# Hymba decoder step: the verdict among the last multiplications, the general pass on SyncE's queue, the first norm's squares behind the first four products

## The chip, the cores and the metric

One core of a Trainium2 chip runs the whole program in one launch. The metric is the device time of a run in microseconds (us). The engines are TensorE (PE; its weight loads are listed as PEld), VectorE (DVE), ScalarE (ACT), GpSimd (POOL) and SyncE (SP, which here only issues transfers). An engine's name with a q (POOLq, SPq) stands for its sequencer: branches, semaphores, register loads, DMA issues.

## The reference

A decoder layer for 264 token columns (a prompt of 256 and 8 single new tokens), model width 2048, all in float32:

```python
h = h + 0.5 * swiglu(rmsnorm(h, norm_ffn1), ffn1_gate, ffn1_up, ffn1_down)
mix, C_f, n_f, m_f, buf = mixing_block(rmsnorm(h, norm_mix), w_in, b_gates, ...)
h = h + mix
h = h + 0.5 * swiglu(rmsnorm(h, norm_ffn2), ffn2_gate, ffn2_up, ffn2_down)
y = rmsnorm(h, norm_final)
```

with `swiglu(x, wg, wu, wd) = (silu(x @ wg) * (x @ wu)) @ wd` (inner width 5504) and `rmsnorm(x, g) = x * rsqrt(mean(x*x) + 1e-6) * g`. The mixing block is a chunkwise mLSTM with four heads beside a gated short convolution. Outputs are y and the new states.

## The kernel before, in words

**Layout.** Activations lie transposed: the 2048 features are 16 blocks of 128 partitions, `h[0]` to `h[15]`, each 128 x 264 float32; two neighbours share one tile, `hpair[i]`, 128 x 528. Every large product goes through the weights in pieces of up to 8 blocks of 128 x 128 (512 KB of float32).

**Two passes.** `hymba_step` records the program twice. The first pass splits each float32 operand into two float16 parts and takes three products per block (`three`, L224 to L226: high·high, high·low, low·high). It also keeps sums that tell whether the numbers stayed in float16's range: `watch` reduces 16 columns of each product into a column of `stat`, `watch_norm` reduces each norm's sums into `squares`, and `judge` compares them with bounds. The single number `bad` is loaded by all five engines (L109); if it is not 0, the second, general pass is run (L110). With these inputs it is skipped: each engine takes the branch over the general pass's instructions.

**A weight piece's way.** `fetch` issues the load on SP's queue (`wraw`), ACT rounds it to float16 (`whi`, L178), DVE makes the rest (`wlo = wraw - whi`, L186), and PE takes both. Six buffers each stand between them; `product` keeps five pieces ahead. Nothing is reordered by a scheduler: instructions stand on each engine in the order in which the code is written (`manual_schedule`), except that `at(n, f)` puts `f` off by n steps of `tick`, of which each product makes two (its start and its half).

**The start.** The first four products (gate and up of blocks 0 and 1) are taken together by `products4` while x arrives: nine groups, two with one feature block and seven with two; a group of two holds 2 x 4 x 3 = 24 matmuls. `ahead` loads a group's h, cuts x = h·gain into two float16 parts (ACT then DVE, 264 columns each), and squares h for the first norm: even blocks on ACT (L376), odd ones on POOL (L378), summed on POOL into `acc` (L382). After the four products `norm.finish` sums `acc` over the partitions with a matmul against ones (L353), `rsqrt` makes the norm's factor, and DVE scales the finished products by it. Here F0 to F8 name the nine groups, and W9, W10, ... the 512 KB pieces behind them, two to a product.

**The end.** `ffn("2")` closes with 16 down products. After each, `done(kb)` adds to the final norm's squares; the last calls `nf.finish`. Then DVE multiplies the 16 blocks of h by the factor (L480), SP stores them (L482, L484), and behind that come `watch_norm`, two `judge`s, the matmul of the verdicts (L492) and the cast to `bad` (L497). A program ends with a barrier of all engines (L1066): SP waits there for all transfers, POOL gathers the others and clears the semaphores.

**Queues.** Weights, h and y go by SP's queue, `h[0]` and `vecs` by ACT's. The small transfers of the mixing block and `bg` are issued by POOL (software-driven queue), in both passes.

Of the kernel before, what the change touches and what calls it, by code (L numbers as in the profile page):

```python
# [8 lines left out]
F32 = mybir.dt.float32  # L9
F32R = mybir.dt.float32r  # L10
F16 = mybir.dt.float16
AF = mybir.ActivationFunctionType
# [3 lines left out]
KB = D // 128  # L16
# [98 lines left out]
def step(ctx: ExitStack, tc: tile.TileContext, a: dict, bad=None):  # L115
# [6 lines left out]
    AHEAD = 5 if half_size else 2  # L122

# [16 lines left out]
    nc.gpsimd.dma_start(bg, a["bg"])  # L140
# [142 lines left out]
    if half_size:  # L283
        stat = const.tile([128, NSTAT], F32, name="stat")
        nc.gpsimd.memset(stat, 2.0 * SUMS[0])
        squares = const.tile([128, 8], F32, name="squares")
# [69 lines left out]
    class Norm:  # L356
# [5 lines left out]
        def block(self, kb, by_act=False):  # L362
            self.cut(kb)
            self.square(kb, by_act)
# [7 lines left out]
        def square(self, kb, by_act=False):  # L372
            new = self.acc is None
            sq = t264("acc", 1) if new else t264("sq")
            if by_act:
                nc.scalar.activation(sq, h[kb], AF.Square)  # L376
            else:
                nc.gpsimd.tensor_tensor(sq, h[kb], h[kb], op=ALU.mult)  # L378
# [14 lines left out]
    def ffn(layer, norm, done, start=None):  # L393
        with tc.tile_pool(name=f"act_{norm.tag}", bufs=1) as apool:
            first = True
            for half, blocks in enumerate(HALVES):
                act = {}
                for i, j in enumerate(blocks):
                    if start is not None and j < 2:
                        if j == 0:  # L400
                            ps4 = start()
                        pg, pu = ps4[2 * j : 2 * j + 2]
                    else:
                        pg = product((layer, "g", j), norm.x, range(KB))
                        pu = None
# [8 lines left out]
                    if pu is None:  # L414
                        pu = product((layer, "u", j), norm.x, range(KB))
# [19 lines left out]
    def ahead(part):  # L435
# [5 lines left out]
        for kb in range(k0, k0 + n):  # L441
            n1.block(kb, kb % 2 == 0)
# [9 lines left out]
        bank=bank, at=at, tick=tick, watch=watch, high=high, low=low, PART=PART, s3=s3,  # L452
# [6 lines left out]
    def done(kb):  # L459
# [12 lines left out]
    def judge_early():  # L472
        early.append(len(stats))
        judge(stat[:, : early[0]], SUMS)

# [9 lines left out]

    if half_size:
        watch_norm(nf.ssum)
        judge(stat[:, early[0] : len(stats)], SUMS)
        judge(squares, SQUARES)
        ps = bank()[:1, :1]  # L490
        for i, v in enumerate(verdicts):
            nc.tensor.matmul(  # L492
                ps, v, ones[:, :1], start=(i == 0), stop=(i == len(verdicts) - 1)
            )
        some = const.tile([1, 1], F32, name="some")
        nc.vector.tensor_scalar(some, ps, 128.0 * len(verdicts) - 0.5, None, op0=ALU.is_lt)
        nc.vector.tensor_copy(bad, some)  # L497


def mix(tc, a, nm, n2, h, e):  # L500
# [6 lines left out]
    bank, at, tick = e["bank"], e["at"], e["tick"]  # L507
# [39 lines left out]
    nc.gpsimd.dma_start(m0, a["m0"])  # L547

    buf = mp.tile([128, 8, NS, 2], F32, name="buf")
    nc.gpsimd.dma_start(buf, a["conv0"])  # L550
# [25 lines left out]
    def gates_rows():  # L576
# [7 lines left out]
        nc.gpsimd.dma_start(drows, rows)  # L584
        nc.gpsimd.dma_start(a["m_p"], rows[:, 1, SEQ - 1 : SEQ])

    def gates_by_token():
# [17 lines left out]
        nc.gpsimd.dma_start(a["m_s"], ms)  # L605
# [5 lines left out]
    class Head:  # L611
        def __init__(self, hd):
            self.hd = hd
            self.n = mp.tile([8, HD], F32, tag="n", name="n")
            nc.gpsimd.dma_start(self.n, a["n0"][:, hd])
# [37 lines left out]
        def load_decays(self):  # L653
            self.bc = mp.tile([128, 2, SEQ], F32, tag="bc", name="bc", bufs=1)
            nc.gpsimd.dma_start(self.bc, drows[self.hd].partition_broadcast(128))
# [118 lines left out]
        def keep_state(self):  # L774
# [3 lines left out]
            nc.gpsimd.dma_start(a["c_p"][:, self.hd], co)  # L778
# [12 lines left out]
        def sample_vectors(self):  # L791
# [23 lines left out]
            nc.gpsimd.dma_start(self.dr, r)  # L815
# [270 lines left out]
```

## Time and profile before

| | |
|---|---|
| median of 3 runs | 1876.56 us (1875.29 to 1877.31) |
| the profiled execution's own time | 1874.37 us |
| its span, first to last instruction | 1872.5 us |
| PE busy | 1830.6 us, 98% |
| DVE, ACT, POOL busy | 64%, 46%, 8% |

The profiled execution is 1.87 us longer than its span, and 2.2 us shorter than the median of the runs. Times inside the trace count from the span's start. An instruction's duration runs from its start to its end, and neighbours on an engine overlap a little, so that start-to-start distances are shorter than durations.

### The profile page before, as it was taken

How to read it: one execution, taken by the hardware profiler on the slowest of the kernel's cores; microseconds unless marked ns; L12 is line 12 of the kernel's file. 1: busy time of each engine (PE TensorE's matmuls, PEld its weight loads, DVE VectorE, ACT ScalarE, POOL GpSimd, SP SyncE). 2: the span in 40 equal slices, each digit the busy share in tenths (PEclk: the TensorE clock that was granted, in tenths of full speed). 3: DMA queues.
4: the chain of work that ended last, by engine and by line, in shares of the span. 5: the costliest groups of instructions: out<-in, count | busy, mean ns of one | idle time of the engine just before them, and what ended most of it. 6: DMA issues, size and time to landing. Idle time of an engine off the chain costs nothing.

```text
span 1872.5 us, 38560 instructions
## 1 busy us (share of the span) xinstructions
PE 1830.6 (98%) x16107; PEld 1586.8 (85%) x16107; DVE 1191.9 (64%) x1910; ACT 859.6 (46%) x1211; POOL 146.8 (8%) x219
## 2 busy tenths in 40 slices
PE   8999999999999999999999899999999999999994
PEld 6888888888888888888888688888888888888884
DVE  8666655466666557888888666666655456666453
ACT  6444443344444444656566645444443434444441
POOL 5000000000000211211211021000000000000110
PEclk9999999999999999999999999999999999999997
DMA  7666565656565555878778565656656656655551
GB/s 263 215 198 200 185 206 187 207 189 198 190 199 181 201 187 189 280 236 290 263 236 296 167 206 188 207 188 196 202 189 192 206 187 197 202 188 186 197 192 54
DMA packets 114714, 381.11 MB, mean 204 GB/s; under 512 B 14797, under 2 KB 19997, under 8 KB 114529
## 3 DMA queue, kind: packets, MB, share of 16 engines
q1 hardware_dynamic: 106048, 350.79, 57.4%
q0 software_dynamic: 8192, 27.57, 4.3%
q8 instruction: 128, 2.10, 0.4%
q14 instruction: 58, 0.47, 0.1%
q10 hardware_dynamic: 288, 0.19, 0.1%
HBM read 366.72 MB, written 11.78 MB: 202 GB/s over the span
## 4 chain that ended last, share of the span: by engine, by line
PE 82%; DVE 9%; issue 3%; ACT 2%; DMA 2%; POOL 0%; SPq 0%; DVEq 0%; ACTq 0%; POOLq 0%
PE ps L225 27%; PE ps L224 27%; PE ps L226 27%; DVE wlo L186 3%; DMA rb<-dr 1%; DVE cs L842 1%; ACT whi L178 1%; DVE jk L853 1%; ACT jk L861 1%; ACT L329 0%; DMA wraw<-in_w1gu 0%; DVE x L186 0%; DVE qkv L514 0%; DVE h L480 0%; DVE rs_q L338 0%
## 5 line engine op out<-in xcount | busy, mean ns | idle before, releaser
L186 DVE SCALAR_TENSOR_TENSOR wlo<-wraw,whi 128x1024 f16<-128x1024 f32 (+2 forms) x683 | 787.7, 1194 | 233.7 <-ACT whi L178 233.5
L226 PE MATMUL ps<-x,wlo 128*128 128x264 f16 x2752 | 759.6, 276 | 4.3 <-DVE wlo L186 4.3
L224 PE MATMUL ps<-x,whi 128*128 128x264 f16 x2752 | 759.6, 276 | 1.6 <-ACT whi L178 1.4
L225 PE MATMUL ps<-x,whi 128*128 128x264 f16 x2752 | 759.6, 276 | 0.0
L178 ACT ACTIVATE whi<-wraw 128x1024 f16<-128x1024 f32 (+2 forms) x683 | 664.9, 1016 | 165.5 <-PE ps L225 159.3
L226 PEld LDWEIGHTS <-wlo 128*128 128x128 f16 (+1 forms) x5296 | 518.6, 98 | 84.4 <-DVE wlo L186 6.5
L225 PEld LDWEIGHTS <-whi 128*128 128x128 f16 (+1 forms) x5296 | 518.6, 98 | 81.2 <-issue 1.8
L224 PEld LDWEIGHTS <-whi 128*128 128x128 f16 (+1 forms) x5296 | 518.6, 98 | 80.2 <-ACT whi L178 2.1
L224 PE MATMUL ps<-a,whi 128*128 128x264 f16 x1376 | 379.8, 276 | 0.0
L225 PE MATMUL ps<-a,whi 128*128 128x264 f16 x1376 | 379.8, 276 | 0.0
L226 PE MATMUL ps<-a,wlo 128*128 128x264 f16 x1376 | 379.8, 276 | 0.0
L224 PE MATMUL ps<-xm,whi 128*128 128x264 f16 (+1 forms) x912 | 252.3, 277 | 0.0
L225 PE MATMUL ps<-xm,whi 128*128 128x264 f16 (+1 forms) x912 | 252.3, 277 | 0.0
L226 PE MATMUL ps<-xm,wlo 128*128 128x264 f16 (+1 forms) x912 | 252.2, 276 | 0.0
L178 ACT ACTIVATE a<-tc 128x264 f16<-128x264 f32 x86 | 36.4, 423 | 295.0 <-DVE tc L418 292.6
L413 ACT ACTIVATE tb<-ta 128x264 f32<-128x264 f32 x86 | 36.3, 423 | 224.0 <-DVE ta L410 222.1
L425 DVE SCALAR_TENSOR_TENSOR h<-ps,h 128x264 f32<-128x264 f32 x64 | 27.7, 433 | 159.5 <-PE ps L226 159.5
L417 DVE TENSOR_TENSOR tc<-ps,rstd 128x264 f32<-128x264 f32 x86 | 37.1, 432 | 94.5 <-PE ps L226 94.5
L378 POOL TENSOR_TENSOR acc<-h 128x264 f32<-128x264 f32 x3 | 1.9, 626 | 1177.0 <-DVE stat L294 589.1
L410 DVE TENSOR_TENSOR ta<-ps,rstd 128x264 f32<-128x264 f32 x86 | 37.2, 432 | 60.4 <-PE ps L226 60.2
L186 DVE SCALAR_TENSOR_TENSOR a<-tc,a 128x264 f16<-128x264 f32 x86 | 37.3, 433 | 42.2 <-ACT a L178 42.2
L382 POOL TENSOR_TENSOR acc<-acc,sq 128x264 f32<-128x264 f32 x59 | 55.2, 936 | 6.4 <-ACT sq L376 1.8
(184 smaller groups left out, 864.8 us busy)
## 6 DMA issues: line engine op xcount, KB each, us to landing
wraw<-in_w2gu SPq DMA_DIRECT2D x172, 512.0 KB, 4.9
wraw<-in_w1gu SPq DMA_DIRECT2D x171, 512.0 KB, 4.8
wraw<-in_win SPq DMA_DIRECT2D x112, 512.0 KB, 5.5
wraw<-in_w1d SPq DMA_DIRECT2D x80, 448.0 KB, 4.1
wraw<-in_w2d SPq DMA_DIRECT2D x80, 448.0 KB, 4.0
wraw<-in_wout SPq DMA_DIRECT2D x32, 512.0 KB, 4.5
rb<-dr POOLq DMA_DIRECT2D x16, 513.0 KB, 10.2
wraw<-in_w1d SPq DMA_DIRECT2D x16, 512.0 KB, 4.4
```

Source lines behind the costliest of these rows:

```text
L178: nc.scalar.activation(dst, src, AF.Copy, scale=scale)
L186: nc.vector.scalar_tensor_tensor(dst, src, scale, hi, op0=ALU.mult, op1=ALU.subtract)
L224: nc.tensor.matmul(ps, wh, xk[:, 0, :], start=first, stop=False)
L225: nc.tensor.matmul(ps, wh, xk[:, 1, :], start=False, stop=False)
L226: nc.tensor.matmul(ps, wl, xk[:, 0, :], start=False, stop=last)
L382: nc.gpsimd.tensor_tensor(self.acc, self.acc, sq, op=ALU.add)
L410: nc.vector.tensor_tensor(zg, pg, norm.r, op=ALU.mult)
L413: nc.scalar.activation(sg, zg, AF.Silu)
L417: nc.vector.tensor_tensor(zu, pu, norm.r, op=ALU.mult)
L425: nc.vector.scalar_tensor_tensor(h[db], ps, 0.5 / (sw * sa[layer]), h[db], op0=ALU.mult, op1=ALU.add)
L842: nc.vector.scalar_tensor_tensor(c[:, b, eb], rb[:, b, HD : 2 * HD], self.v[eb][:, col : col + 1], c[:, b, eb], op0=ALU.mult, op1=ALU.add,)
L853: nc.vector.tensor_tensor(jk, c, rb[:, :, :HD].unsqueeze(2).to_broadcast([128, 2, 2, HD]), op=ALU.mult)
```

## The change

Three things are changed.

1. `start`: `ahead` now only cuts x. The squares are recorded behind the four products as `square_pairs`: eight ACT squares of whole pairs (128 x 528) into two tags of tiles, with seven POOL additions of that size. The two products of block 2 are recorded ahead of `norm.finish`, whose column sum is now two matmuls (one for each half of the pair). `h[0]` is loaded by SP, ahead of the first weights, and `vecs` is the first on ACT's queue.
2. `queue`: the general pass issues its small transfers on SP's queue; the first pass still uses POOL's.
3. The verdict: `squares` is judged in `judge_early`, the final norm's sum is watched by one ACT instruction that adds a column to `stat` in place of two DVE reductions into `squares`, and `judge_late` stands between the sixth and the seventh of the 16 multiplications.

```diff
+    queue = nc.gpsimd if half_size else nc.sync
...
-    nc.gpsimd.dma_start(bg, a["bg"])
+    queue.dma_start(bg, a["bg"])
...
-    nc.scalar.dma_start(h[0], a["xt"][:, 0, :])
     nc.scalar.dma_start(vecs, a["vecs"])
+    nc.sync.dma_start(h[0], a["xt"][:, 0, :])
...
+        def square_pairs(self, pool, pairs):
+
+            for i in pairs:
+                tag = f"sq{min(i, 1)}"
+                sq = pool.tile([128, 2, T], F32, tag=tag, name=tag, bufs=1 + 2 * min(i, 1))
+                nc.scalar.activation(sq, hpair[i], AF.Square)
+                if i == 0:
+                    self.acc = sq
+                else:
+                    nc.gpsimd.tensor_tensor(self.acc, self.acc, sq, op=ALU.add)
...
-            self.ssum = column_sums(self.acc, *rest)
+            acc = [self.acc] if len(self.acc.shape) == 2 else [self.acc[:, i] for i in range(2)]
+            self.ssum = column_sums(*acc, *rest)
...
+                    if first and start is not None:
+
+                        ps4 = start()
+                        for n, ps in enumerate(ps4):
+                            early[n // 2, "gu"[n % 2]] = ps
+                        for step, pairs in ((0, (0, 1)), (1, (2, 3)), (1.5, (4, 5)), (2, (6, 7))):
+                            at(step, norm.square_pairs, apool, pairs)
+                        tick(0)
+                        for which in "gu":
+                            early[2, which] = product((layer, which, 2), norm.x, range(KB))
+                    pg = gate_up(j, "g")
...
-            n1.block(kb, kb % 2 == 0)
+            n1.cut(kb)
...
+            if half_size:
+                j = len(stats)
+                stats.append(j)
+                nc.scalar.activation(
+                    t264("ta"), nf.ssum, AF.Copy, scale=2.0**10, accum_out=stat[:, j : j + 1]
+                )
...
+        judge(squares, SQUARES)
+
+    def judge_late():
+        judge(stat[:, early[0] : len(stats)], SUMS)
+        ps = bank()[:1, :1]
+        for i, v in enumerate(verdicts):
+            nc.tensor.matmul(
+                ps, v, ones[:, :1], start=(i == 0), stop=(i == len(verdicts) - 1)
+            )
+        some = const.tile([1, 1], F32, name="some")
+        nc.vector.tensor_scalar(some, ps, 128.0 * len(verdicts) - 0.5, None, op0=ALU.is_lt)
+        nc.vector.tensor_copy(bad, some)
...
+        if half_size and kb == 5:
+            judge_late()
...
-        nc.gpsimd.dma_start(drows, rows)
-        nc.gpsimd.dma_start(a["m_p"], rows[:, 1, SEQ - 1 : SEQ])
+        queue.dma_start(drows, rows)
+        queue.dma_start(a["m_p"], rows[:, 1, SEQ - 1 : SEQ])
...
```

The other small transfers of the mixing block change in the same way. How the instructions stand, at three places (a name before `<-` is the tile that is written; brackets name the engines or queues that an instruction waits for):

On ACT at the start, before: a group's x, the square of its even block between the two cuts, and the weights.

```order
L178 ACTIVATE x_337<-h_83,gains 128x264 [waits DMAHW5_49]
L376 ACTIVATE sq<-h_83 128x264 [waits Pool_49]
L178 ACTIVATE x_343<-h_83,gains 128x264
L178 ACTIVATE whi<-wraw 128x1024 [waits DMAHW6_49,DVE_49,PE_49]
L178 ACTIVATE x_380<-h_84,gains 128x264 [waits DMAHW7_49]
L376 ACTIVATE sq<-h_84 128x264 [waits Pool_49]
```

And now, on the same engine from the last weights that `products4` fetches (W13):

```order
L179 ACTIVATE whi<-wraw 128x1024 [waits DMAHW7_49,DVE_49,PE_49]
L387 ACTIVATE sq_472<-h_78 128x528
L387 ACTIVATE sq_474<-h_79 128x528
L387 ACTIVATE sq_477<-h_80 128x528
L387 ACTIVATE sq_480<-h_81 128x528
L179 ACTIVATE whi<-wraw 128x1024 [waits DMAHW0_49,DVE_49,PE_49]
L387 ACTIVATE sq_514<-h_82 128x528 [waits Pool_49]
L387 ACTIVATE sq_517<-h_83 128x528 [waits Pool_49]
L387 ACTIVATE sq_544<-h_84 128x528 [waits Pool_49]
L387 ACTIVATE sq_547<-h_85 128x528 [waits Pool_49]
L179 ACTIVATE whi<-wraw 128x1024 [waits DMAHW1_49,DVE_49,PE_49]
```

The squares have moved from between the cuts to behind W13's rounding; four stand on either side of W14's, and the last four wait for POOL to give their tiles back.

On DVE at the end, before: all multiplications, then the verdict.

```order
L480 TENSOR_TENSOR h_85<-h_85,rstd 128x264 [waits Activation_49]
L304 TENSOR_REDUCE squares<-ps 128x1 x2
L312 TENSOR_SCALAR ok<-stat 128x9 [waits DVE_49]
L313 SCALAR_TENSOR_TENSOR ok<-stat,ok 128x9 [waits DVE_49]
L317 TENSOR_REDUCE verdict_23238<-ok 128x1 [waits DVE_49]
L312 TENSOR_SCALAR ok<-squares 128x8 [waits DVE_49]
L313 SCALAR_TENSOR_TENSOR ok<-squares,ok 128x8 [waits DVE_49]
L317 TENSOR_REDUCE verdict_23243<-ok 128x1 [waits DVE_49]
L496 TENSOR_SCALAR some<-ps 1x1 [waits PE_49]
L497 CAST bad<-some 1x1 [waits DVE_49]
L109 TENSOR_LOAD bad [waits DVE_49]
```

And now, on the same engine:

```order
L516 TENSOR_TENSOR h_80<-h_80,rstd 128x264 x2
L313 TENSOR_SCALAR ok<-stat 128x10 [waits DVE_49,Activation_49]
L314 SCALAR_TENSOR_TENSOR ok<-stat,ok 128x10 [waits DVE_49]
L318 TENSOR_REDUCE verdict_23205<-ok 128x1 [waits DVE_49]
L509 TENSOR_SCALAR some<-ps 1x1 [waits PE_49]
L510 CAST bad<-some 1x1 [waits DVE_49]
L516 TENSOR_TENSOR h_81<-h_81,rstd 128x264 x2
L516 TENSOR_TENSOR h_82<-h_82,rstd 128x264 x2
L516 TENSOR_TENSOR h_83<-h_83,rstd 128x264 x2
L516 TENSOR_TENSOR h_84<-h_84,rstd 128x264 x2
L516 TENSOR_TENSOR h_85<-h_85,rstd 128x264
```

One judgement instead of two is left at the end, and ten multiplications stand behind the cast to `bad`.

On POOL at the program's end, before, the last instructions of the general pass, and behind the first branch what an engine runs that has skipped it (the first `ISA` adds to eight semaphores of the software-driven queue what the skipped transfers would have added; the second belongs to the closing barrier):

```order
L378 TENSOR_TENSOR sq<-h_23301 128x264 [waits DVE_49]
L382 TENSOR_TENSOR acc<-acc,sq 128x264 [waits Pool_49]
L110 UNCONDITIONAL_BRANCH
L110 ISA [waits Pool_49,DMASW4_49,DMASW5_49,DMASW3_49,DMASW6_49,DMASW2_49,DMASW7_49,DMASW1_49,DMASW0_49]
L110 UNCONDITIONAL_BRANCH
L1066 ISA [waits barrier_Pool_Activation_PE_DVE_SP_gather]
```

And now, on the same engine:

```order
L376 TENSOR_TENSOR sq<-h_23278 128x264 [waits DVE_49]
L380 TENSOR_TENSOR acc<-acc,sq 128x264 [waits Pool_49]
L110 UNCONDITIONAL_BRANCH
L110 UNCONDITIONAL_BRANCH [waits Pool_49]
L1091 ISA [waits barrier_Pool_Activation_PE_DVE_SP_gather]
```

The addition to the eight semaphores is gone, as the general pass has no transfer on that queue any more.

## Rows read from the trace of the kernel before

**Rows 1.** The page's first part: busy time (share of the span) and instructions.

```profile
PE 1830.6 (98%) x16107; PEld 1586.8 (85%) x16107; DVE 1191.9 (64%) x1910; ACT 859.6 (46%) x1211; POOL 146.8 (8%) x219
```

**Rows 2.** PE's waits, 6 to 32 us: us in total, times, longest.

```profile
PE ps L226 <- DVE wlo L186: 4.3, 8, 0.9
```

**Rows 3.** Groups by form on DVE, 10 to 31 us: count | busy us, mean ns.

```profile
L186 DVE SCALAR_TENSOR_TENSOR x<-h,gains,x 128x264 f16<-128x264 f32 x12 | 11.2, 971 | 0.0
L186 DVE SCALAR_TENSOR_TENSOR wlo<-wraw,whi 128x1024 f16<-128x1024 f32 x7 | 11.1, 1583 | 0.5 <-ACT whi L178 0.5
```

**Rows 4.** Groups by form on POOL, 10 to 31 us.

```profile
L382 POOL TENSOR_TENSOR acc<-acc,sq 128x264 f32<-128x264 f32 x13 | 16.3, 1254 | 1.0
```

**Rows 5.** Groups by form on DVE, 45 to 400 us, where POOL is idle.

```profile
L186 DVE SCALAR_TENSOR_TENSOR wlo<-wraw,whi 128x1024 f16<-128x1024 f32 x107 | 127.0, 1221 | 41.1 <-ACT whi L178 41.1
...
L186 DVE SCALAR_TENSOR_TENSOR a<-tc,a 128x264 f16<-128x264 f32 x22 | 9.5, 434 | 10.8 <-ACT a L178 10.8
```

**Rows 6.** L382 from 1200 us on; L1059 (the program's first instructions): ns min/median/max.

```profile
L382 POOL TENSOR_TENSOR acc<-acc,sq x14: 740/744/748, 1748.9 to 1841.1; 128x264 f32<-128x264 f32 x14
...
L1059 POOLq INC_SWDGE_SEM  x1: 27/27/27, 0.2 to 0.2; - x1
L1059 POOL MEMSET const-float32-0.0<- x1: 98/98/98, 0.3 to 0.3; 128x1 f32 x1
...
L1059 POOLq DRAIN  x1: 182/182/182, 0.4 to 0.4; - x1
```

**Rows 7.** Timeline of PE: start us, us, instruction, idle before it.

```profile
11.30 0.29 PE L226 MATMUL ps<-x,wlo 128*128 128x264 f16 x1 [0.86 <-DVE wlo L186]
...
33.91 0.61 PE L353 MATMUL ps<-acc,ones 128*128 128x264 f32 x2
34.35 0.28 PE L224 MATMUL ps<-x,whi 128*128 128x264 f16 x1
```

**Rows 8.** Timeline of ACT: the rounding of group F2's weights.

```profile
8.93 1.06 ACT L178 ACTIVATE whi<-wraw 128x1024 f16<-128x1024 f32 x1 [0.24 <-DMA wraw<-in_w1gu]
```

**Rows 9.** A stretch of the start: busy us, granted clock, DMA share, GB/s.

```profile
6.00:24.00 18.00, 14.70 (x122) 11.36 (x122) 17.10 (x19) 13.79 (x27) 15.53 (x16) 1.00 1.07 371
```

**Rows 10.** Groups by form on ACT: the mixing block's square of 528 columns.

```profile
L869 ACT ACTIVATE sq<-ha 128x528 f32<-128x528 f32 x4 | 2.5, 630 | 0.0
```

**Rows 11.** Timeline of DVE, 1850 us to its last instruction.

```profile
1850.64 5.59 DVE L480 TENSOR_TENSOR h<-h,rstd 128x264 f32<-128x264 f32 x16
...
1856.83 0.16 DVE L312 TENSOR_SCALAR ok<-stat 128x9 f32<-128x9 f32 x1
...
1857.42 0.17 DVE L312 TENSOR_SCALAR ok<-squares 128x8 f32<-128x8 f32 x1
...
1858.45 0.14 DVE L497 CAST bad<-some 1x1 int32<-1x1 f32 x1
```

**Rows 12.** Timeline of SP, from 1855 us: the last three stores of y.

```profile
1854.88 1.71 SPq L484 DMA_DIRECT2D out_yt<-h  x3
```

**Rows 13.** L110, the branch and what follows it: ns, first and last start us.

```profile
L110 SPq EVENT_SEMAPHORE  x8: 17/17/17, 1863.2 to 1863.7; - x8
...
L110 SPq COMPARE_BRANCH  x1: 45/45/45, 1859.5 to 1859.5; - x1
...
L110 POOLq INC_SWDGE_SEM  x1: 1716/1716/1716, 1863.7 to 1863.7; - x1
```

**Rows 14.** L1066, the closing barrier: ns, first and last start us.

```profile
L1066 SPq EVENT_SEMAPHORE  x14: 17/28/28, 1865.3 to 1872.5; - x14
...
L1066 POOLq DRAIN  x3: 46/98/6271, 1865.4 to 1872.2; - x3
L1066 SPq DRAIN  x3: 7/7/7, 1866.1 to 1871.9; - x3
```

**Rows 15.** Stretches of the mixing block's end, columns as in rows 9.

```profile
1036.70:1039.50 2.80, 0.04 (x1) 0.00 (x0) 2.36 (x3) 2.78 (x4) 0.00 (x0) 1.00 0.06 12
1039.70:1043.00 3.30, 0.00 (x0) 0.00 (x0) 2.76 (x8) 1.50 (x4) 0.00 (x0) 0.50 0.83 278
```

More of the change, by code (lines that the diff above doesn't have):

```diff
@@ L285, in step @@
         nc.gpsimd.memset(stat, 2.0 * SUMS[0])
-        squares = const.tile([128, 8], F32, name="squares")
+        squares = const.tile([128, 6], F32, name="squares")
     def watch(ps, rows=None):
@@ L360, in __init__, with block @@
             self.tag, self.col, self.x, self.acc = tag, col, [None] * KB, None
-        def block(self, kb, by_act=False):
+        def block(self, kb):
             self.cut(kb)
-            self.square(kb, by_act)
+            self.square(kb)
         def cut(self, kb):
@@ L394, in ffn, with gate_up @@
         with tc.tile_pool(name=f"act_{norm.tag}", bufs=1) as apool:
+            early = {}
+            def gate_up(j, which):
+                return early.pop((j, which), None) or product((layer, which, j), norm.x, range(KB))
             first = True
@@ L398, in ffn @@
                 for i, j in enumerate(blocks):
[L399 to L405, printed above, removed]
+                    if first and start is not None:
[8 more added lines that the diff above has]
+                    pg = gate_up(j, "g")
                     if first:
@@ L413, in ffn @@
                     nc.scalar.activation(sg, zg, AF.Silu)
-                    if pu is None:
-                        pu = product((layer, "u", j), norm.x, range(KB))
+                    pu = gate_up(j, "u")
                     zu = t264("tc")
@@ L451, in step @@
         product=product, split=split, rsqrt=rsqrt, column_sums=column_sums, t264=t264,
-        bank=bank, at=at, tick=tick, watch=watch, high=high, low=low, PART=PART, s3=s3,
+        bank=bank, at=at, tick=tick, queue=queue, watch=watch, high=high, low=low, PART=PART, s3=s3,
         out_scale=1.0 / (sw * s3),
@@ L484, in step @@
             nc.sync.dma_start(a["yt"][:, kb - 1 : kb + 1, :], hpair[kb // 2])
[L486 to L497, printed above, removed]
+        if half_size and kb == 5:
+            judge_late()
 def mix(tc, a, nm, n2, h, e):
@@ L546, in mix @@
     m0 = mp.tile([8, 4], F32, name="m0")
-    nc.gpsimd.dma_start(m0, a["m0"])
+    queue.dma_start(m0, a["m0"])
     buf = mp.tile([128, 8, NS, 2], F32, name="buf")
-    nc.gpsimd.dma_start(buf, a["conv0"])
+    queue.dma_start(buf, a["conv0"])
     ua = mp.tile([128, 8, SEQ + 2 + 3 * NS], F32, name="ua")
@@ L614, in __init__ @@
             self.n = mp.tile([8, HD], F32, tag="n", name="n")
-            nc.gpsimd.dma_start(self.n, a["n0"][:, hd])
+            queue.dma_start(self.n, a["n0"][:, hd])
             at(4, self.load_decays)
@@ L777, in keep_state @@
                 nc.scalar.copy(co[:, db, :], pc[:, : HD + 1])
-            nc.gpsimd.dma_start(a["c_p"][:, self.hd], co)
+            queue.dma_start(a["c_p"][:, self.hd], co)
         def samples(self):
@@ L848, in sample_terms @@
             rb, c = self.rb[n], self.c[n]
-            nc.gpsimd.dma_start(
+            queue.dma_start(
                 a["c_s"][2 * n : 2 * n + 2, self.hd].rearrange("b p e d -> p b e d"), c
@@ L972, in mix @@
     nc.scalar.copy(cvs, uas[:, :, :, 1:3])
-    nc.gpsimd.dma_start(a["conv_p"], cvp)
-    nc.gpsimd.dma_start(a["conv_s"], cvs)
+    queue.dma_start(a["conv_p"], cvp)
+    queue.dma_start(a["conv_s"], cvs)
     inner.close()
```

21 lines of the change are left out of this document (9 added, 12 removed).

## The prediction

> **What bounds the kernel now.** I read the page first: PE is busy for 98% of the span [rows 1], so only what makes PE wait, and what lies ahead of its first or behind its last matmul, can move the time. I then asked for PE's waits, stretch by stretch, and for the sequencers' instructions at the end. The change touches two such places; the order of the instructions in between is the same.
>
> At the start PE waits eight times for DVE's `wlo`, 4.3 us in all [rows 2]. The forms on DVE say why: in that stretch a group costs DVE one `wlo` of 1.58 and two x of 0.97, 3.5 us together [rows 3], while PE needs 24 matmuls x 0.1137 (1830.6 us over 16107, [rows 1]) = 2.7 us. The same `wlo` takes 1.22 elsewhere, and the same two-input form on 264 columns 0.43 [rows 5], so DVE's own work is 1.22 + 2 x 0.43 = 2.1 us. What differs is POOL: its addition takes 0.74 later on [rows 6] and 1.25 here [rows 4]. The two slow each other, and the first norm's squares make DVE the bound of this stretch.
>
> At the end the last of DVE's work is the cast to `bad`, over at 1858.45 + 0.14 = 1858.59 [rows 11], but the span ends at 1872.5. The rows of L110 and L1066 fill those 14 us: the branch, 3.7 us without an instruction on SP (1859.5 to 1863.2), eight semaphore additions to 1863.7, POOL's INC_SWDGE_SEM of 1.72 [rows 13], and then a DRAIN on POOL of 6.27 us from 1865.4 to 1871.7, for which the barrier waits [rows 14].
>
> **The change part by part: the start.** With the squares gone from the loop, DVE's 2.1 us and ACT's rounding and two cuts lie under PE's 2.7. The loads could be the next bound: a group is 776 KB, and the queue moves 371 GB/s with the DMA engines busy throughout [rows 9], 2.1 us, also below 2.7. So from F2's low parts on (11.30, [rows 7]; its weights land at 8.93, [rows 8], and are still the gate) PE runs on: 166 matmuls to the end of F8, 11.30 + 18.9 = 30.2 us, and block 2's two products (96) end at 41.1. `h[0]` now stands ahead of the first weights on SP's queue; as F2's load is held up by bytes and the bytes are the same, I take nothing for it, with 0 to 0.5 us of loss as its ends.
>
> The squares come back as a chain in front of the column sum. ACT has them behind W13's rounding. From F3 to W13 there are 6 x 776 + 5 x 512 = 7216 KB, 7.39 MB, at 371 GB/s 19.9 us: W13 lands at 28.9. Its rounding takes 1.06 [rows 8], and the first two squares 0.63 each [rows 10]: POOL begins at 31.2. An addition of 528 columns isn't in the trace. It lies between one of 264 columns, 0.74, and two, 1.49; I take two less one instruction's least cost, 0.10 (the one-column memset of [rows 6]), 1.4. Seven: 9.8, to 41.0. Beside them DVE runs three `wlo` (W14 to W16). A POOL addition beside a busy DVE takes 1.25/0.74 = 1.69 times as long [rows 4, 6], so POOL loses 1.58 x (1 - 1/1.69) = 0.65 us per `wlo`, 1.9 in all: the sum is complete at 42.9 or 43.0, and PE has waited some 1.9 us for it. The Trainium skill ("GPSIMD Engine Reference", section "Performance versus the Vector engine") has a dearer unit but a cheaper sum here: 4497 ns for 2048 columns, an estimate of 1.16 us for 528, by which PE would wait 0.3 us and the start would gain 2.9. No row here shows that size.
>
> A column sum held PE from 33.91 to 34.35, 0.44 us [rows 7]; there are two now, 0.88. PE then starts block 3 at 43.9. Before, block 2 began at 34.35, so block 3 stood at 34.35 + 10.9 = 45.25. **Gain at the start: 1.3 us.** Its ends: no wait at the sum, 41.1 + 0.9 = 42.0, 3.3; and a loss of 0.4 (rival 2). Behind the sum DVE has three blocks to scale instead of two, before it makes W17's low part. I count some 2.3 us per block (four times 0.43 by [rows 5], and the turns to ACT in between), with the factor ready 2 us behind the sum: W17 is ready about 10.8 us behind it, just when PE, with W13 to W16 in hand, asks for it. I take no loss; half a microsecond would not surprise me.
>
> **The verdict.** DVE's multiplications go at 5.59/16 = 0.35 [rows 11]. Six end at 1852.74. The judgement from its first row to the end of the cast took 1858.59 - 1856.83 = 1.76 us with two judgements; one is 1857.42 - 1856.83 = 0.59, so 1.17 are left: `bad` stands at 1853.91, 4.7 us earlier, and the ten multiplications behind it end at 1857.4 instead of 1856.2. Queued behind the wait for PE's matmul are those ten, and SP's stores behind them: that is the 1.2 us the early verdict costs. SP's last store ended at 1854.88 + 1.71 = 1856.59 [rows 12], 0.36 behind the last multiplication; now 1857.8. SP has loaded `bad` in the meantime and branches at once. `squares` is judged during the last down products, three small instructions where PE is the bound. ACT's second reading of the sum lies between the factor's first step and the wait for it, with 2 us to spare; without that cover it would cost its own half microsecond.
>
> **The general pass's queue.** POOL's addition to eight semaphores (1.72 us) is no longer recorded. I hold that the DRAIN of 6.27 us right behind it waits for that very addition: the program's other DRAINs on POOL take 0.05 to 0.18 us [rows 6, 14], and no transfer of that queue is under way. What speaks against it is that the INC_SWDGE_SEM at the start, 27 ns, has a DRAIN of 0.18 behind it [rows 6]; but that one adds to no semaphore.
>
> Then SP is last: branch at 1857.8, 3.7 us to its first semaphore (1861.5), 0.5 for eight of them, 0.8 for the barrier's list of waits (1865.3 to 1866.1, [rows 14]), and 0.8 from the end of POOL's DRAIN to the end of the span (1871.7 to 1872.5): 1863.6. **Gain at the end: 8.9 us**, of which 7.2 by the queue (SP going on at 1863.7 would end at 1865.3) and 1.7 by the verdict.
>
> **Sum.** 1.3 + 8.9 = 10.2 us. The profiled execution took 1874.37; it would take 1864.2. It lies 2.2 below the median of the runs, so the median goes from 1876.56 to 1866.4.
>
> **Rivals.** (1) *No wait at the column sum*: POOL is quicker than 1.4 per addition, or W13 lands earlier. For it: the 0.10 taken off for the second half of an addition is the least it could be. The start gains 3.3, the median is 1864.4. The Trainium skill's figure for the addition ("GPSIMD Engine Reference", the section above) points this way.
>
> (2) *POOL stands still while a `wlo` runs.* Then three `wlo` cost 3 x 1.22 = 3.7 instead of 1.9, the sum is complete at 44.7, PE starts block 3 at 45.6, a loss of 0.4; the median is 1868.1. Against it: in the loop DVE's own 2.1 us and POOL's two additions alone, 1.5, would already fill the 3.5 us, and POOL has a square to make besides. The Trainium skill ("SBUF — State Buffer", section "Who interferes with whom") states this as its single rule: the port pair of VectorE and GpSimd is locked for a whole instruction, and a VectorE instruction with two SBUF inputs contends with a GpSimd instruction that reads. By that rule the start loses 0.4, by the rows it gains 1.3. The trace agrees that they slow each other, not that they exclude each other.
>
> (3) *The DRAIN stays.* POOL reaches its first semaphore 4.6 us behind `bad`, as SP did (1858.59 to 1863.2), so at 1858.5; 6.27 and 0.8 on top give 1865.6. The end gains 6.9, the median is 1868.4. The short DRAIN at the start is for it, the position right behind the addition against it.
>
> (4) *Slower: the additions on POOL hold up the column sum for so long that both gains are eaten.* PE's wait would have to grow by 10.2 + 3.8 us, 2 us on each of the seven additions: it decides from 3.4 us per addition. A long wait has a second price: where PE stood idle from 1036.7 the granted clock was 1.00 for 2.8 us and then 0.50, 1.2 GHz instead of 2.4 [rows 15]. Against it: beside a fully busy DVE 264 columns took 1.25, so 528 stay under 2.5.
>
> (5) *The change does nothing at either place*: other waits close the gaps, 1876. The order of the instructions speaks against it.
>
> **How the numbers follow.** The forecast 56%, rival 1 17%, rival 2 12%, rival 3 10%, rival 4 2%, rival 5 3%. The likeliest gives 1866.4. The range reaches from rival 1 with a quicker branch (1862.5) to rivals 2 and 3 together with the half microseconds left out above (1870.5). A measurement of this kernel can tell about 0.2%, 3.8 us, from no change: faster 0.95, same 0.03, slower 0.02.
>
> **What would show it.** In the new trace: no waits of PE for `wlo` between 14 and 30 us, and the nine groups over by 30.2; POOL's additions near 1.4 us alone and 2 beside DVE; a wait of PE at the column sum of about 2 us; `bad` some 3.5 us ahead of the last multiplication; no INC_SWDGE_SEM at L110, POOL's DRAINs all under 0.2 us, and SP last in the barrier, with about 6 us between the last multiplication and the span's end instead of 16. I am wrong if the DRAIN stays, if PE waits over 4 us at the sum, or if W17 leaves a new gap near 54 us.

## The result and the profile after

The changed kernel takes 1867.07 us (median of 5 runs, 1865.00 to 1868.02) against 1876.56 (5 runs, 1875.29 to 1877.31): ratio 0.9946, 95% interval 0.9933 to 0.996, some 9.5 us faster. The profiled execution took 1868.02 us with a span of 1866.2.

What PE waits for at the start (0 to 70 us; total, times, longest), where [rows 2] had eight waits for `wlo`:

```profile
PE ps L354 <- POOL sq L391: 2.0, 1, 2.0
PE ps L225 <- ACT whi L179: 1.3, 2, 0.9
PE ps L227 <- DVE wlo L187: 1.2, 2, 0.9
```

The waits of the loop are gone (the last is over before 14 us); one of 2.0 us at the column sum is new. On DVE, 10 to 31 us, by form (to set beside [rows 3]), and the additions on POOL (ns min/median/max, first and last start):

```profile
L187 DVE SCALAR_TENSOR_TENSOR wlo<-wraw,whi 128x1024 f16<-128x1024 f32 x11 | 13.5, 1226 | 3.4 <-ACT whi L179 2.1 <-PE ps L226 1.0
L187 DVE SCALAR_TENSOR_TENSOR x<-h,gains,x 128x264 f16<-128x264 f32 x12 | 5.3, 487 | 0.0
```

```profile
L391 POOL TENSOR_TENSOR sq<-sq,sq x7: 1301/1311/2162, 32.2 to 41.4; 128x528 f32<-128x528 f32 x7
```

With POOL silent, a `wlo` takes 1226 ns instead of 1583 and x 487 instead of 971. POOL's additions take 1.31 us alone and 2.16 where a `wlo` is in their way. What the wait does to PE is in its timeline and in a table of stretches (length, busy time of PE, PEld, DVE, ACT and POOL with counts, then granted clock, DMA share, GB/s):

```profile
43.57 1.88 PE L354 MATMUL ps<-sq,ones 128*128 128x264 f32 x4 [2.02 <-POOL sq L391]
45.24 0.43 PE L225 MATMUL ps<-x,whi 128*128 128x264 f16 x1
45.46 0.43 PE L226 MATMUL ps<-x,whi 128*128 128x264 f16 x1
```

```profile
41.30:43.50 2.20, 0.24 (x3) 0.00 (x0) 2.20 (x2) 1.08 (x1) 2.15 (x1) 1.00 0.09 15
43.50:45.20 1.70, 1.63 (x4) 1.12 (x5) 1.09 (x1) 0.00 (x0) 0.01 (x1) 0.60 0.76 234
45.30:47.20 1.90, 1.90 (x10) 1.31 (x9) 1.13 (x3) 1.69 (x2) 0.00 (x0) 0.50 0.62 209
47.30:50.00 2.70, 2.70 (x26) 2.35 (x25) 2.07 (x8) 0.84 (x2) 0.00 (x0) 1.00 0.17 65
```

PE stood for 2 us at a clock of 1.00 (2.4 GHz); behind that, during the column sums, the clock falls to 0.50 (1.2 GHz). The two column sums take 1.67 us (43.57 to 45.24), not 0.88, and the nine matmuls behind them come 0.22 apart instead of 0.11.

At the end, DVE's last instructions, then the branch and the closing barrier (columns as in [rows 13, 14]):

```profile
1852.57 2.15 DVE L516 TENSOR_TENSOR h<-h,rstd 128x264 f32<-128x264 f32 x6
...
1855.48 0.14 DVE L509 TENSOR_SCALAR some<-ps 1x1 f32<-1x1 f32 x1 [0.28 <-PE ps L505]
1855.66 0.14 DVE L510 CAST bad<-some 1x1 int32<-1x1 f32 x1
1855.73 3.50 DVE L516 TENSOR_TENSOR h<-h,rstd 128x264 f32<-128x264 f32 x10
```

```profile
L110 SPq EVENT_SEMAPHORE  x8: 17/17/17, 1864.0 to 1864.5; - x8
...
L110 POOLq COMPARE_BRANCH  x1: 45/45/45, 1856.5 to 1856.5; - x1
...
L110 POOLq EVENT_SEMAPHORE  x1: 17/17/17, 1857.0 to 1857.0; - x1
...
L110 SPq COMPARE_BRANCH  x1: 50/50/50, 1860.6 to 1860.6; - x1
```

```profile
L1091 SPq EVENT_SEMAPHORE  x14: 17/28/28, 1864.6 to 1866.1; - x14
...
L1091 POOLq DRAIN  x3: 50/98/6271, 1857.0 to 1865.9; - x3
L1091 SPq DRAIN  x3: 7/7/7, 1865.3 to 1865.6; - x3
```

Three things are to be seen. No INC_SWDGE_SEM is left at L110. **The DRAIN of 6.271 us is still there**, to the nanosecond as long as before; it now starts at 1857.0 and is over at 1863.3, two microseconds before SP has gone through its waits. And POOL passes the branch in half a microsecond (1856.5 to 1857.0), where POOL and SP both took about 4 before. SP is last: branch at 1860.6, first semaphore 3.4 us later, list of waits to 1865.3, end at 1866.2.

To compare kernels by stretch I use two marks that all have: DVE's addition of a down product to h (`h<-ps`), the first and the last of the 64 on its line, and the span's end. Before and after:

```profile
L425 DVE SCALAR_TENSOR_TENSOR h<-ps,h x64: 432/433/433, 258.0 to 1847.0; 128x264 f32<-128x264 f32 x64
```

```profile
L443 DVE SCALAR_TENSOR_TENSOR h<-ps,h x64: 431/433/434, 259.1 to 1848.9; 128x264 f32<-128x264 f32 x64
```

The start up to the first mark took 1.1 us longer (259.1 against 258.0), the middle 0.8 longer (1589.8 against 1589.0), the end 8.2 shorter (1866.2 - 1848.9 = 17.3 against 1872.5 - 1847.0 = 25.5). The two profiled executions differ by only 6.3 us, since the one of before lay 2.2 below its median and this one 0.9 above.

### The profile page after: what moved, and what is told of

Same layout as the page of the kernel before. It is cut to its first block, busy times and chain, and to the rows that moved or that the text cites. A ratio compares the mean times of both kernels' runs of the same rounds, so it can differ in the third digit from the quotient of the medians.

```text
span 1866.2 us, 38542 instructions
## 1 busy us (share of the span) xinstructions
PE 1833.9 (98%) x16109; PEld 1586.6 (85%) x16109; DVE 1185.5 (64%) x1908; ACT 863.1 (46%) x1213; POOL 134.4 (7%) x203
## 4 chain that ended last, share of the span: by engine, by line
PE 84%; DVE 8%; issue 2%; ACT 2%; DMA 2%; POOL 1%; SPq 0%; DVEq 0%; ACTq 0%; POOLq 0%
PE ps L225 28%; PE ps L226 28%; PE ps L227 28%; DVE wlo L187 3%; DMA rb<-dr 1%; ACT whi L179 1%; DVE cs L867 1%; DMA wraw<-in_w1gu 1%; DVE jk L878 1%; POOL sq L391 1%; ACT jk L886 0%; PE ps L354 0%; DVE rs_q L339 0%; ACT L330 0%; DVE h L516 0%
## 5 line engine op out<-in xcount | busy, mean ns | idle before, releaser
L295 DVE TENSOR_REDUCE stat<-ps 128x1 f32<-128x16 f32 x310 | 51.3, 165 | 0.0
## 6 DMA issues: line engine op xcount, KB each, us to landing
rb<-dr POOLq DMA_DIRECT2D x16, 513.0 KB, 10.3
```

The source lines that it names most:

```text
L295: nc.vector.tensor_reduce(stat[r, j : j + 1], ps[r, T - SEEN : T], axis=mybir.AxisListType.X, op=ALU.add, apply_absolute_value=True,)
```

## Experiments

"Start", "middle" and "end" are the three stretches between these marks, in us, of the profiled execution; ratios are medians against the kernel before.

| kernel | start | middle | end | ratio (95% interval) |
|---|---|---|---|---|
| before | 258.0 | 1589.0 | 25.5 | 1 |
| changed | 259.1 | 1589.8 | 17.3 | 0.9946 (0.9933 to 0.996) |
| changed, again | 257.0 | 1591.4 | 17.7 | 0.9960 (0.9946 to 0.9973) |
| queue alone | 258.4 | 1591.1 | 20.3 | 0.9979 (0.9969 to 0.9989) |
| verdict alone | 258.0 | 1591.9 | 20.5 | 0.9973 (0.9962 to 0.9983) |
| verdict and queue | 258.5 | 1590.7 | 17.3 | 0.9967 (0.9955 to 0.9979) |
| start alone | 258.3 | 1590.3 | 25.5 | 0.9990 (0.9981 to 0.9999) |
| changed, additions on DVE | 254.8 | 1589.4 | 17.4 | 0.9947 (0.9934 to 0.9961) |
| changed, h[0] on ACT's queue | 256.7 | 1590.4 | 16.8 | 0.9954 (0.9940 to 0.9968) |
| changed, two stores by ACT | 257.3 | 1591.0 | 16.8 | 0.9947 (0.9933 to 0.9960) |
| changed, longer POOL list | 257.1 | 1589.9 | 18.1 | 0.9957 (0.9942 to 0.9972) |
| the three single edits together | 254.3 | 1589.0 | 16.9 | 0.9936 (0.9922 to 0.9949) |

The middle is the same work in all of these and still varies from 1589.0 to 1591.9; this spread is as large as one part of the change. The stretch is the better measure of a part, the ratio of the whole.

**The queue alone.** The kernel before with

```diff
+    queue = nc.gpsimd if half_size else nc.sync
...
-        nc.gpsimd.dma_start(drows, rows)
+        queue.dma_start(drows, rows)
```

and so for the other transfers of GpSimd. 

> The kernel before, with nothing changed but the queue of the general pass's transfers (SyncE instead of GpSimd, in the general pass alone). Theory: GpSimd's DRAIN of 6.27 us at the end of the program stays, of the same length, and begins earlier, because GpSimd's list of the general pass is now short: its branch takes about 0.5 us instead of 4, and the addition to eight semaphores (1.72 us) is gone. It then ends some 5.7 us earlier, the end of the span 5.7 to 6.2 us earlier: 1870.4 to 1870.9 us against 1876.6. Rival A, the prediction's: the DRAIN goes away with the addition and SyncE is last, 7.2 us: 1869.4, with all of GpSimd's DRAINs under 0.2 us. Rival B: the DRAIN stays and so does the pause of 4 us at GpSimd's branch; only the addition's 1.7 us and some of the eight semaphores are saved: 1874.4 to 1874.9.

The end takes 20.3 us, a gain of 5.2. The median is 1871.85 us, 3.9 under the kernel before measured beside it and 1 us above what was expected; the profile's middle is 2.1 longer than that of before. The closing barrier and the branch:

```profile
L1067 POOLq DRAIN  x3: 98/198/6271, 1862.3 to 1869.4; - x3
```

```profile
L110 POOLq COMPARE_BRANCH  x1: 45/45/45, 1861.7 to 1861.7; - x1
...
L110 POOLq EVENT_SEMAPHORE  x1: 17/17/17, 1862.2 to 1862.2; - x1
```

The addition is gone, the DRAIN isn't: it begins right behind the branch, and the span's end follows it. The prediction's cause for the DRAIN falls here. The gain comes from POOL getting to it earlier, by 1.7 us (the addition) and by the pause, 0.5 instead of 4. Counted from the last addition to h, the DRAIN ends 5.7 us earlier, as the theory had it; what follows it took 1.3 us here (1868.5 to 1869.8) and 0.8 before.

**The verdict alone**: `judge_late` behind the sixth multiplication, everything else as before. 

> The kernel before, with nothing changed but the verdict (its judgement behind the sixth of the last multiplications, ACT's reading of the last sum); the general pass keeps its transfers on GpSimd's queue. Theory: the verdict comes 4.7 us earlier, and behind it GpSimd's pause at the branch (4 us), the addition to eight semaphores (1.7) and the DRAIN (6.27) follow unchanged and are last: 1871.9 us, a gain of 4.7. Rival: SyncE is last, because the early verdict makes the last multiplications and stores 1.2 us later and GpSimd's rows are hidden; the gain is then over 6 us, 1870 or less. If the DRAIN is longer by what it begins earlier (waiting for something else that ends at its own time), there is no gain: 1876.6.

```profile
L110 POOLq COMPARE_BRANCH  x1: 50/50/50, 1857.5 to 1857.5; - x1
...
L110 POOLq INC_SWDGE_SEM  x1: 1716/1716/1716, 1861.6 to 1861.6; - x1
```

```profile
L1074 POOLq DRAIN  x3: 46/98/6271, 1863.4 to 1870.2; - x3
```

POOL's chain (pause of 3.7, addition, DRAIN) is whole and begins earlier; the end is 5.0 shorter, as the theory had it (4.7).

**Verdict and queue**, the changed kernel with the old start. 

> The changed kernel with the start of the kernel before: verdict and queue together. Theory: GpSimd's DRAIN stays but begins 3.5 us ahead of the last multiplication and is hidden; SyncE is last. The end gains 8.2 to 8.9 us: 1867.7 to 1868.4. The two parts alone (5.7 to 6.2 and 4.7) add up to more, 10.4 to 10.9, since both shorten one chain, GpSimd's, until SyncE's is the longer. With the whole change at 1867.1 the start would then be worth 0.6 to 1.3. Rival: the start lost some 2 us, so without it the time is under 1866.

The end is 17.3 us, a gain of 8.2: less than the 5.2 and 5.0 of the parts together, because from some point on SP's path, which the queue doesn't shorten, is the longer one. POOL's DRAIN runs from 1857.4, SP's closing semaphores come at 1863.8. The median of 1869.8 lies 1.4 above the upper end of what was expected, with a middle that is 1.7 us longer than in the profile of before; the end alone is as expected.

**The start alone**, and **the changed kernel once more** as a control. 

> The kernel before, with nothing changed but the start (the squares as pairs behind the first four products, the first block of x loaded on SyncE's queue). Theory: TensorE waits no more in the loop, but some 2 us for the sum of the squares, after which its granted clock is 0.5 for 3.4 us; with the slower column sums this gives the gain of the loop back, and block 3 starts where it did before: 1875.6 to 1877.6 us, no difference that can be measured. Rival, the prediction's own sum: 1.3 us faster, 1875.3, with the clock at 1.0 behind the wait. Rival 2: slower by 1.9 us (1878.5), as the last work of the profiled execution after the whole change came 1.9 us later than before.

> The changed kernel once more, unaltered, as the control beside the others: 1867 us, ratio 0.995 to the kernel before. Its profile shows whether the fall of the granted clock behind the wait at the first column sum comes in every execution (theory of the first profile: yes, 3.4 us at 0.5 and 0.8 us lost at the sums) or only in some, as the profile of the start alone, which waited 2.7 us at a clock of 1.0, lets one think.

The wait at the column sum was 2.7 us in the first of them (where W13's weights landed 0.9 later) and 1.4 in the second, and in neither did the clock fall behind it. The start alone:

```profile
41.90:44.40 2.50, 0.00 (x0) 0.00 (x0) 2.50 (x2) 1.40 (x2) 2.42 (x2) 1.00 0.06 11
44.50:45.40 0.90, 0.90 (x4) 0.77 (x5) 0.90 (x1) 0.00 (x0) 0.00 (x0) 1.00 0.86 264
45.50:48.00 2.50, 2.50 (x24) 2.18 (x23) 1.72 (x6) 1.76 (x2) 0.00 (x0) 1.00 0.68 233
```

So my reading of the first profile, that the wait brings the clock down each time, was wrong: of the eight profiles with this wait (1.1 to 2.7 us) one shows the fall. Where it came it cost 1.7 us, 0.7 at the sums (1.67 us, against 0.99 behind the control's wait) and 1.0 in the nine matmuls behind them. The first mark is at 257.0 in the control; the old start has 258.0 to 258.5 in four profiles, the new one, with h[0] on SP's queue and POOL's additions, 257.0 to 259.1 in five, 257.7 in the mean. That is a gain of 0.5 us, less than either group's spread of profiles would let one call certain; the ratio of the start alone (0.2 to 3.6 us faster) doesn't contradict it.

**The additions on DVE.**

```diff
-                    nc.gpsimd.tensor_tensor(self.acc, self.acc, sq, op=ALU.add)
+                    nc.vector.tensor_tensor(self.acc, self.acc, sq, op=ALU.add)
```

> The changed kernel, but the seven additions of the squares go to VectorE instead of GpSimd. VectorE has nothing to do in much of this stretch; one addition of two pairs should take it about twice 0.43 us. Theory: the start's gain in the loop is eaten at the column sum by GpSimd's chain of 11 us, so without it TensorE doesn't wait there (0 instead of 2.0 to 2.7 us), the granted clock can't fall behind that wait, the two column sums take 0.9, and the first down product, whose addition to h began at 259.06 us in the changed kernel's profile and at 258.31 with the start alone, comes at 255.7 to 256.3. Time: 2 to 3 us under the changed kernel in the same call, 1864 to 1865 if that is at 1867. Rival: the start is not held there but by the loads (weights and x arrive at their own time), and the time stays within 0.5 us of the changed kernel. Rival 2: VectorE's own low parts come late behind the additions, a new wait of TensorE for wlo takes over; the time is the same or longer, with the wait in the list.

```profile
L391 DVE TENSOR_TENSOR sq<-sq,sq x7: 701/708/709, 32.3 to 38.2; 128x528 f32<-128x528 f32 x7
```

```profile
PE ps L227 <- DVE wlo L187: 1.2, 2, 0.9
PE ps L225 <- ACT whi L179: 1.2, 2, 1.0
```

The sum is ready at 38.9, more than 2 us before PE asks for it; the wait is gone and no other takes its place. PE starts block 3 at 42.00, the first mark is at 254.8, 2.9 us below the mean of the five with POOL's additions. So POOL's chain, and not the loads, held the start: block 3 at 42.0 is the prediction's own end for "no wait at the sum". The time, 1866.3, is 1.6 under the control measured beside it, where 2 to 3 were expected, and within the spread of either.

**h[0] on ACT's queue again**, as before the change. 

> The changed kernel, but the first block of x is loaded on ACT's queue ahead of the vectors, as in the kernel before. The prediction took 0 to 0.5 us of loss for the move. Theory: the move costs some 0.6 us at the second group (its weights stood at 9.5 us instead of 8.9), but this is made up by the first matmuls (4.99 us instead of 6.34); the loop ends at the same time within 0.5 us, and the time is that of the changed kernel within what the measurement can tell. Rival: the move costs its 0.6 us or more to the end, so this version is 0.6 to 1 us faster. Rival 2: the move gains 1 us (TensorE starts earlier), so this version is 1 us slower.

F2's weights are rounded earlier (ACT ends at 10.05 us; at 10.3 to 10.9 in five profiles with h[0] on SP's queue), PE starts later (6.10 against 4.9 to 5.3), and the first mark is at 256.7, 1.0 below the mean of the five and 0.2 below the best of them. One profile and a ratio of 0.9954 don't decide between the theory and the first rival. The version with all three edits, below, has h[0] on ACT's queue too, and its first mark is 0.5 below that with the additions on DVE alone; both pairs point to the first rival.

**Two of the last stores by ACT.** 

> The changed kernel, but two of the five last pair stores of y are issued by ACT instead of SyncE. Theory: SyncE is last at the end, and of its path 0.9 to 1.3 us are stores that queue up behind its reading of the verdict and behind one issue of 1.66 us; with three stores instead of five it issues the last one at once behind the last multiplication, and the span ends 0.8 us earlier: from the last addition to h to the end of the span 16.5 us instead of 17.3. Rival: ACT is then last (its pause at the branch, 2.7 us, begins behind its last store), the span ends at the same time, 17.3, or later. Either is less than the measurement of the time can tell; the profile decides.

The end is 16.8 us. But it is 16.8 in the profile with h[0] on ACT's queue too, whose stores are all SP's, so the half microsecond can't be put down to this. The stores' issues (ns min/median/max), changed kernel first:

```profile
L520 SPq DMA_DIRECT2D out_yt<-h x7: 332/383/1659, 1854.1 to 1860.1; - x7
```

```profile
L521 SPq DMA_DIRECT2D out_yt<-h x5: 332/333/886, 1853.4 to 1858.7; - x5
L521 ACTq DMA_DIRECT2D out_yt<-h x2: 338/348/357, 1856.6 to 1858.0; - x2
```

With fewer stores one of SP's, the last, is still a slow one (0.89), so the expected 0.8 don't come. Before the change none of these seven took more than 0.333.

**A longer list on POOL.** Instructions that are never run:

```diff
+    if not half_size:
+        pad = const.tile([128, 1], F32, name="pad")
+        for _ in range(200):
+            nc.gpsimd.memset(pad, 0.0)
```

> The changed kernel with 200 more one-column memsets on GpSimd in the general pass, which isn't run: no instruction that runs is added. Theory: GpSimd's pause at the branch was 4 us before and in the kernels that keep the general pass's transfers on its queue, and 0.5 us where they are gone, because the branch passes over a shorter list; with 200 more instructions the pause of about 4 us comes back, the DRAIN of 6.27 us begins 3.5 us later and ends some 1.3 us after SyncE is ready: the span ends 1 to 1.5 us later than in the changed kernel (18.3 to 18.8 us behind the last addition to h, against 17.3). Rival: the pause comes with the transfers (their queue) and not with the list's length; it stays at 0.5 us and the end at 17.3.

```profile
L110 POOLq COMPARE_BRANCH  x1: 50/50/50, 1854.6 to 1854.6; - x1
...
L110 POOLq EVENT_SEMAPHORE  x1: 17/17/17, 1857.9 to 1857.9; - x1
```

```profile
L1095 POOLq DRAIN  x3: 50/98/6271, 1858.0 to 1864.8; - x3
L1095 SPq DRAIN  x3: 7/7/7, 1863.5 to 1864.5; - x3
```

The pause is back, 3.3 us, without one transfer. The long DRAIN begins at 1858.0 and ends at 1864.2, behind SP's first, 1863.5: POOL is last again, and the end is 18.1 instead of 16.8 to 17.7. So a longer skipped list is enough to bring the pause back, without any transfer.

**No transfer, or one transfer, of GpSimd's.** In the first version all of the first pass's small transfers go to SP as well (`queue = nc.sync`); in the second the first of them, `bg`, is GpSimd's. 

> The changed kernel with the first pass's small transfers too on SyncE's queue, so that GpSimd issues no transfer in the whole program. A look at GpSimd's DRAIN of 6.27 us, whose cause the prediction had wrong. Theory: the DRAIN has to do with GpSimd's transfers (those of the first pass are the only ones left in the changed kernel) and falls under 0.2 us here. Rival: it comes with the end of the program on GpSimd whatever its transfers, and is 6.27 us here too. The span's end moves by neither, since SyncE is last: 17.3 us behind the last addition to h. The small transfers may stand in the way of the weights on SyncE's queue, so the time may be some us longer.

> As the version whose first pass issues its small transfers on SyncE, but the very first of them (bg, 256 bytes, loaded at the program's start) is GpSimd's again: one transfer of GpSimd in the whole program. Theory 1: GpSimd's last DRAIN is a fixed price of having used that queue at all, 6.27 us. Theory 2: it grows with the number of its transfers (or of bytes): some 0.1 us with one. The time is that of the version on SyncE, 1930 us, either way.

With none, then with one:

```profile
L1091 POOLq DRAIN  x3: 34/45/82, 1917.8 to 1927.0; - x3
```

```profile
L1091 POOLq DRAIN  x3: 44/93/140, 1917.5 to 1927.2; - x3
```

The DRAIN behind the branch is 0.05 us with no transfer, 0.14 with one, 6.27 with all of the first pass's. It is the price of GpSimd's own transfers, paid once at the end, and it grows with them; whether with their number or their bytes these runs don't tell. Taking them away is no remedy: on SP's queue the time is 1929.9 us, 54 more than before, where some microseconds were expected. The middle takes 1650.5 us instead of some 1590; which of these transfers holds up what there was not followed.

**The three single edits together.** 

> The changed kernel with the three edits that were tried singly: the additions of the squares on VectorE, the first block of x on ACT's queue, two of the last stores by ACT. Theory: the first down product's addition to h at 254.3 to 255 us (256.7 to 259.1 in the five profiles of the changed start with GpSimd's additions), and 16.8 us from the last addition to h to the end instead of 17.3: 2.5 to 3.5 us under the changed kernel, 1863.5 to 1865, ratio 0.993 to 0.9935. Rival: what the start gains is lost again to the granted clock in the mixing block, and the time is within 1 us of the changed kernel, 1866 to 1868.

1863.59 us (1861.81 to 1864.54), ratio 0.9936: this is the fastest version, 12.6 us under the kernel before measured beside it and 3.5 under the first median of the changed kernel. Start 254.3 and end 16.9 are where they were expected. The interval overlaps that of the changed kernel, but the slowest of its five runs is faster than the fastest of the five first runs of the changed kernel, 1865.00. The two were not measured side by side.

## Why the prediction came out as it did

The forecast of 1866.4 was 0.7 under the measured median, and the order of the parts was right: nearly all at the end, little at the start. That the number came out is in part luck. At the end two steps were wrong and cancelled (that POOL's DRAIN goes, and that its pause at the branch stays), and at the start POOL's loss beside DVE was near the forecast by another mechanism. Measured by stretch, the parts make 0.5 + 8.2 = 8.7 us; the medians say 9.5 here and 8.3 for the control.

**The start** (predicted 1.3, measured 0.5 in the mean). The loop went as worked out. W13 came late: its rounding, forecast from 28.9, began at 29.97. h[0] ahead of the weights, taken as nothing, may be part of that, which isn't shown: F2's first rounding stood at 9.52 instead of [rows 8]'s 8.93, and W13's began at 29.32 in both profiles with h[0] back on ACT's queue, at 29.34 to 31.83 in the eight with it on SP's. POOL's chain took 11.34 us where 9.8 + 1.9 = 11.7 were expected: alone its additions follow each other at 1.39 us, as forecast (1.4), and two of them, not three, were held up. So the sum was complete at 43.5 instead of 43.0, and PE waited 2.0 instead of 1.9. An addition took 1.31 us from its start to its end. By the figure of the Trainium skill ("GPSIMD Engine Reference", section "Performance versus the Vector engine") it is an estimated 1.16 us, too little here; the same section's advice to leave elementwise work to VectorE agrees with the traces, 0.71 against 1.31 us. Not in the sum was the clock: 1.7 us in one of eight profiles. It had been seen as a price in the fourth rival alone, for a much longer wait.

**Rival 2**, POOL standing still under a `wlo`, is what happened, but DVE stands still under an addition too: the two take turns. So the rival's price was wrong. DVE and POOL in the changed kernel:

```profile
34.14 1.82 DVE L187 SCALAR_TENSOR_TENSOR wlo<-wraw,whi 128x1024 f16<-128x1024 f32 x1 [1.86 <-ACT whi L179]
40.17 2.19 DVE L187 SCALAR_TENSOR_TENSOR wlo<-wraw,whi 128x1024 f16<-128x1024 f32 x1 [4.21 <-ACT whi L179]
42.28 2.31 DVE L187 SCALAR_TENSOR_TENSOR wlo<-wraw,whi 128x1024 f16<-128x1024 f32 x1
```

```profile
33.57 1.31 POOL L391 TENSOR_TENSOR sq<-sq,sq 128x528 f32<-128x528 f32 x1
34.96 2.16 POOL L391 TENSOR_TENSOR sq<-sq,sq 128x528 f32<-128x528 f32 x1
39.97 1.30 POOL L391 TENSOR_TENSOR sq<-sq,sq 128x528 f32<-128x528 f32 x1
41.35 2.16 POOL L391 TENSOR_TENSOR sq<-sq,sq 128x528 f32<-128x528 f32 x1
```

The `wlo` of 34.14 begins while an addition is at work, and ends at 35.96, 1.08 us behind that addition's end (34.88). The next addition, begun at 34.96, ends 1.16 behind the `wlo` (37.12). The later group repeats both distances: the `wlo` of 40.17 ends 1.09 behind the addition of 39.97, the addition of 41.35 ends 1.15 behind that `wlo`, and the last `wlo` 1.08 behind that addition. All eight profiles with these additions on POOL have the same distances, to 0.02 us. So each of the two does nearly all of its own work (1.23 and 1.31) when the other is done, however long they seem to overlap. The kernel before shows the same:

```profile
12.96 1.64 DVE L186 SCALAR_TENSOR_TENSOR wlo<-wraw,whi 128x1024 f16<-128x1024 f32 x1
13.60 1.60 POOL L382 TENSOR_TENSOR acc<-acc,sq 128x264 f32<-128x264 f32 x1
```

This addition ends 0.60 us behind the `wlo`; the seven additions that follow a `wlo` from 10 us on all end 0.60 or 0.61 behind it. The Trainium skill's rule ("SBUF — State Buffer", section "Who interferes with whom") has VectorE and GpSimd lock the port pair for a whole instruction; the trace agrees, but for some 0.15 us of each instruction that the other's doesn't delay (1.23 alone against 1.08, 1.31 against 1.16).

Rival 2 had priced this at three times 1.22. But a `wlo` that has waited for an addition itself holds up the next one for less, 0.86 us (2.16 - 1.31), and the last `wlo` has no addition behind it: 1.7 in all. The forecast's 1.9 came near this from a slowing of both in proportion to their overlap (1.69 times), which the ends above don't show. Its argument against rival 2 charged DVE with all of an addition's 0.74 us; less the 0.15 at either end that doesn't delay the other, some 0.45 are left, and 2.1 + 2 x 0.45 leave room for POOL's square within the 3.5.

**The verdict** came as predicted, `bad` 3.4 us ahead of the last multiplication (predicted 3.5), whose end lay 6.7 us behind the start of the first one (6.8 worked out).

**The queue: the step that failed** is "the DRAIN waits for that very addition". It doesn't; rival 3 (10%) was right in that the DRAIN stays. What made the forecast hold all the same is something that it had not seen, and so luck: with the short list POOL's pause at the branch falls from 4 to 0.5 us. Rival 3 had assumed SP's 4 us for it, hence its end at 1865.6. POOL in fact began the DRAIN at 1857.0, so it is hidden, and SP is last, as the forecast had it for another reason. The parts were valued in the wrong proportion too: queue alone 7.2 predicted, 5.2 measured; the verdict 1.7 on top, 3.0 measured.

**SP at the end.** From the last multiplication to the span's end 6.2 us were predicted (1857.4 to 1863.6), and it took 7.0 (1859.23 to 1866.2): SP issued its last store 0.9 us late, because one store took 1.66 us. This is the 0.7 by which the end's gain fell short of 8.9.

**W17** left no gap: from the start of block 3 to the first mark it was 212.8 us in the control, and an estimated 212.7 before (258.0 less the prediction's 45.25). **The difference to the median** (2.2) was carried over as it stood; the middle of before was with 1589.0 us one of the two shortest here, 1.4 below the mean of the other eleven, so most of these 2.2 us lay there.

## What to carry to other kernels

At the end of a program, look at the sequencers, not the engines: a wait that is there to the nanosecond in every trace may belong to work long done, and what helps is to start it earlier, beside something else. A pass that is never run has a price through the length of the list a branch skips, and through the queues it uses. A chain of small additions belongs on the engine that is idle and quick, not on the one that is merely free: the same seven additions took 11.3 us on GpSimd and 6.5 on VectorE (32.35 to 38.87). And before two engines are called slow beside each other, set the ends of their instructions side by side: they may be taking turns.

## What was unexpected of the hardware

- The DRAIN on POOL at the program's end: 0.05, 0.14 and 6.27 us with no, one and all transfers of the first pass, always 6.271 for the same set.
- A branch over a list is passed in 0.5 us on POOL where the general pass's transfers were on another queue, and takes 3.3 us with 200 memsets more (one profile) and 3.7 to 4 with those transfers.
- Additions on GpSimd and two-input instructions on VectorE took turns: an addition that began beside a `wlo` ended 1.15 to 1.17 us behind it (128 x 528) or 0.60 to 0.61 (128 x 264), whatever its start.
- After PE stood idle for 1.1 to 2.7 us at the column sum, the clock fell to 0.50 in one profile of eight, with a wait of 2.0 us, and not in the one with the longest wait.
- While other engines pass the branch, one store issued by SP takes 0.9 to 1.7 us instead of 0.33 to 0.42, in every profile with the early verdict.
